# A convolution module on one core: two chunks instead of three on VectorE, GpSimd's splits and sums moved to VectorE

## The chip, the core and the metric

The kernel runs on one core of a Trainium2 chip. The core has TensorE (matrix products into PSUM), VectorE, ScalarE, GpSimd, and SyncE (SP), which issues the DMA transfers. Each engine works through a queue of its own in program order, and semaphores hold an instruction back until what it needs is done. The metric is the device time of one execution in microseconds; lower is better.

## What is computed

The reference is a two-layer trunk over 512 tokens of 1024 features, all in fp32. Layer 0 has a mixer (spatial gating and neighbourhood attention) and a squared-ReLU channel mixer, layer 1 a Conformer convolution module and another channel mixer. The change touches the convolution module alone:

```python
def conformer_conv(h, w_pw1, b_pw1, w_dw, b_dw, ln_g, ln_b, w_pw2, b_pw2):
    a, gate = jnp.split(h @ w_pw1 + b_pw1, 2, axis=-1)
    y = a * jax.nn.sigmoid(gate)
    y = lax.conv_general_dilated(y, w_dw[:, None, :], window_strides=(1,),
                                 padding=[(CONV_K // 2, CONV_K // 2)],
                                 dimension_numbers=('NWC', 'WIO', 'NWC'),
                                 feature_group_count=CONV_W) + b_dw
    y = jax.nn.silu(layernorm(y, ln_g, ln_b))
    return y @ w_pw2 + b_pw2
```

The convolution is depthwise with 31 taps along the tokens; the layer norm behind it needs the mean and variance over all 1024 channels of each token.

## The kernel before

Features lie on the partitions: the 1024 channels are eight chunks of 128, and a chunk is a tile of 128 x 512 tokens. fp32 products are made from two parts, a rounded high part and the remaining low part: `mm3` (L87 to L90) issues high x high, low weight x high, high weight x low. Weights come as 1 MB tiles (`raw`, two buffers, loaded by SP) and are split in four quarters by `Weights.piece`: ScalarE casts the high part `whi` (L93), and VectorE or GpSimd subtracts it for the low part `wlo` (L94); `el` says which. A tile's next load is issued after its last quarter's split, and `raw` is free when that split is done. `chunk` (L218) issues a chunk's 24 matmuls, then up to two quarters of the next tile, then "side work" for VectorE worth so many microseconds (`work`), then the chunk's evacuation from PSUM.

The side work in this stage is the convolution of some chunks on VectorE: the chunks in `VECTOR_CONV` are convolved by 31 multiply-adds each (a "tap", L1125 and L1128), queued in `aux` and drawn by `work` from two chunks in turn. The other chunks are convolved on TensorE (`conv_steps`, L1152): for those, 16 DMA copies of 67.5 KB on SP's queue (L1140) write shifted copies of the padded chunk `ypad` into four tiles `y` (for chunk 7, ten copies by DMA and six by ScalarE, L1138), GpSimd builds matrices of taps (`conv_weights`, L1148) in two buffers, and 32 matmuls with 32 columns each go through them (64 passes of TensorE in the trace).

`glu(c)` makes chunk c of the gated product: two `chunk` calls of 24 matmuls each, ("g", c) evacuated by ScalarE's sigmoid (L1106), ("a", c) by VectorE into `ypad` (L1116). Chunks 0 and 1 are made before `conv_module` begins. Each convolved chunk is centred on `m0` (the mean over the channels of chunk 0) and added to running sums of values and squares by `take` (L1175 to L1184); GpSimd keeps one set of sums for chunks 0 and 4, VectorE another for the rest, and two additions (L1239) merge them. `sums` (L1248) then turns the running sums into statistics with TensorE, and `normed` (L1270 to L1278) norms the chunks as operands of the last product. The order of all this is the order in which `conv_module` is written; there is no planner.

Of the kernel before, what the change touches and what calls it, by code (L numbers as in the profile page):

```python
# [27 lines left out]
VECTOR_CONV = (1, 2, 3)  # L28

# columns of the packed vectors  # L30
# [12 lines left out]
# columns of the shape constants  # L43
# [6 lines left out]
# window of a query tile of 16 columns: first key column, kind of mask  # L50
# [5 lines left out]
def body(ctx: ExitStack, tc: tile.TileContext, I: dict, out: bass.AP):  # L56
# [11 lines left out]
    def nm(s):  # L68
        uid[0] += 1
        return f"{s}_{uid[0]}"  # L70
# [25 lines left out]
    class Pieces:  # L96
        """a weight tile in four pieces of two rows of blocks"""
# [8 lines left out]
    class Weights:  # L106
        """Weight tiles in the order of their use: loaded and split ahead of it, in pieces."""
# [15 lines left out]
        def piece(self, i, q, el=None):  # L123
            """a quarter of a tile, in its two parts"""
# [50 lines left out]
    def work(us):  # L175
        """emit side work worth about us of VectorE time, from two queues in turn"""
        while aux and us > 0:
            queue = aux[0]
            cost, go = queue.popleft()
            go()  # L180
            us -= cost
            if not queue:
                aux.popleft()
            elif len(aux) > 1:
                aux[0], aux[1] = aux[1], aux[0]

    def steps(m, w, c, acts, evac, t0=0, t1=T, ks=range(KC), every=2):
        """one output chunk; yields every few k"""
# [14 lines left out]
    def together(ms, acts, evac, t0=0, t1=T, ks=range(KC), hook=None):  # L203
        """output chunks side by side, k outermost; ms: (id, weight tile, column)"""
# [13 lines left out]
    def chunk(m, w, c, acts, evac, us, ks=range(KC), t0=0, t1=T, np_=2, el=None):  # L218
        """one output chunk, with side work beside it"""
# [59 lines left out]
    def preload(func):  # L279
        """brings in a function's table ahead of its use"""  # L280
        act.activation(small(1, "pre"), epsc, func)
# [4 lines left out]
    class SumSq:  # L286
        """Running sum of squares over feature chunks."""
# [19 lines left out]
        def flush(self):  # L307
            """the last addition, a step behind its square"""
# [16 lines left out]
    def gain(norm, s):  # L325
        """norm_g * (1 + s)"""
# [4 lines left out]
    def modulate(items, r, alt):  # L331
        """items: (source, gain, shift, hi, lo); one item a step, its low part a step later"""
# [25 lines left out]
    # ================= start =========================================  # L358
# [13 lines left out]
    # silu(c) along the free axis, on every partition  # L372
# [11 lines left out]
    # shift and scale of the first norm, for x and for ctx, a quarter of the features at a time;  # L384
    # each row group of the array holds a quarter of the sum
# [135 lines left out]
    # ================= layer 0: mixer ================================  # L521
# [6 lines left out]
    def perm(t):  # L528
        """the (block, row, column) order of a tile, seen in token order"""
# [23 lines left out]
    def first_v():  # L553
        """the first weights of v, where scores and modulation weights go later"""
# [9 lines left out]
    # ctx, normalised and modulated  # L564
# [85 lines left out]
    # bias of a head over the 48 columns around a query tile, then under the three masks  # L650
# [12 lines left out]
    def head_bias(hd, rows):  # L663
        """the table comes back to front: its rows rise with the query, and are read from the end"""
# [12 lines left out]
    # spatial gating  # L677
# [3 lines left out]
    def gelu2(dst, ps, n):  # L681
        """twice gelu(ps), tanh form"""
# [39 lines left out]
    def spatial(gs):  # L722
        """the gate over the tokens"""
# [23 lines left out]
    # attention, for the two heads of a pair and 16 columns of queries at a time  # L747
# [46 lines left out]
    def weigh(u):  # L794
# [12 lines left out]
        if j == 3:  # L807
            # the reciprocals of the sums, along the free axis
# [73 lines left out]
    # the last of the content, and the mixer's halves as operands of the last projection  # L882
# [33 lines left out]
    def norm_between(acts, evac, ss, norm, l, qs, qc, evac_next, ids, third, ks=range(KC),  # L916
                     between=lambda: None, staged=True):
        """the last four chunks of one product, a norm, and the first four chunks of the next one, by token halves;
        third: where the first weights of the next product go; returns the normed operand"""
# [94 lines left out]
    # ================= channel mixer =================================  # L1014
    def mlp(l, lead, us, tail):
        """lead: norm_between without its consumer; tail: what follows the last but two chunks"""
# [25 lines left out]
        def third():  # L1042
            """eight slots of the hidden layer, before they are needed"""
# [37 lines left out]
    def free_gemv():  # L1081
        """the two buffers of the modulation weights, which are done"""
# [5 lines left out]
    # ================= layer 1: convolution module ===================  # L1088
# [13 lines left out]
    def evac_glu(m, ps, t0, t1):  # L1102
# [19 lines left out]
        if c in VECTOR_CONV:  # L1122
# [8 lines left out]
            aux.append(deque(jobs + [(1.8, lambda: take(c, dve))]))  # L1131
# [13 lines left out]
    def conv_weights(c):  # L1145
        n = len(cv["matrices"]) % 2
        wd = cv["matrices"][c] = cv["wd"][:, n * 1024 : n * 1024 + 1024].rearrange("p (a b) -> p a b", b=32)
# [22 lines left out]
    def take(c, e, t0=0, t1=T):  # L1170
        """centre a chunk on m0 and add it to the engine's sums"""
        m0 = cv["m0"]
        lsum, lsq = cv["sums", e is pool]
        z = zs[c][:, t0:t1]
        e.tensor_tensor(z, z, m0[:, t0:t1], op=ALU.subtract)  # L1175
        if (e is pool) not in cv["begun"]:
            cv["begun"].add(e is pool)
            e.tensor_copy(lsum[:, t0:t1], z)
            act.activation(lsq[:, t0:t1], z, AF.Square)
        else:  # L1180
            sq = slot(cols=t1 - t0, s="sq")
            act.activation(sq, z, AF.Square)
            e.tensor_tensor(lsum[:, t0:t1], lsum[:, t0:t1], z, op=ALU.add)
# [318 lines left out]
```

## Time and profile before

| | us |
|---|---|
| median of three runs | 1203.87 |
| lowest and highest run | 1201.37, 1205.72 |
| span of the profiled execution (its run time is not given apart) | 1200.8 |
| TensorE busy in that span | 1157.8 |
| VectorE, ScalarE, GpSimd busy | 761.0, 474.1, 227.5 |

The span runs from the first to the last instruction of one profiled execution. Times of day in the text are microseconds from its start; the convolution stage lies between about 665 and 812. A row of a timeline merges instructions of one kind that follow each other: start, time from the first start to the last end, engine, line, operation, tiles, count, and in brackets the idle time before it with what ended it. Instructions of one engine overlap a little, so a row's time divided by its count is the pace, while a mean of single durations is somewhat longer. Matmul ends are modelled. The granted clock (PEclk) is the share of TensorE's full clock in that stretch.

### The profile page before, as it was taken

To read this page: it belongs to the slowest core of one execution; us is meant where nothing else is said; L and a number is where in the kernel's file an instruction comes from. 1 tells how busy PE (TensorE), PEld (TensorE's weight loads), DVE (VectorE), ACT (ScalarE), POOL (GpSimd) and SP (SyncE) were. 2 spreads that over 40 slices of the span, in tenths; PEclk is the share of its full clock that TensorE was granted. 3 is DMA by queue.
4 is the path that set the end of the run, shared out by engine and by line. 5 is a ranking of instruction groups with operands and counts; after the bars stand their busy time and mean duration, and the time that the engine had idled before them with its cause. 6 is when DMAs were issued, how large, how long until landed. Compare 5 with 4: busy or idle time off the path is not lost.

```text
span 1200.8 us, 16380 instructions
## 1 busy us (share of the span) xinstructions
PE 1157.8 (96%) x6534; PEld 963.4 (80%) x6534; DVE 761.0 (63%) x1251; ACT 474.1 (39%) x940; POOL 227.5 (19%) x194
## 2 busy tenths in 40 slices
PE   6999999999999999999999999699999999999997
PEld 2688889779988888888889766288988888888887
DVE  4685776557775666665757899877743343443445
ACT  4463445444541331332335332366642242332423
POOL 1240325253200000000012476444200000000001
PEclk8999999999999999999999999799999999999998
DMA  9624444143364455455532415204133222332322
GB/s 366 229 77 162 168 168 142 35 169 112 113 221 178 189 210 199 155 206 208 204 115 75 143 48 163 82 19 141 36 105 106 75 102 105 105 99 77 105 71 70
DMA packets 29836, 160.79 MB, mean 134 GB/s; under 512 B 3968, under 2 KB 7552, under 8 KB 11840
## 3 DMA queue, kind: packets, MB, share of 16 engines
q1 hardware_dynamic: 29760, 159.75, 38.1%
q8 instruction: 51, 0.84, 0.3%
q14 instruction: 25, 0.20, 0.1%
HBM read 152.52 MB, written 2.10 MB: 129 GB/s over the span
## 4 chain that ended last, share of the span: by engine, by line
PE 75%; DVE 7%; DMA 3%; POOL 3%; ACT 3%; issue 2%; DVEq 0%; ACTq 0%; POOLq 0%
PE ps L88 20%; PE ps L89 20%; PE ps L90 20%; PE ps L213 3%; PE ps L210 3%; PE ps L211 3%; DMA graw<-in_wmB_dram 2%; POOL wlo L94 2%; DVE graw L505 1%; PE ps L1159 1%; DMA raw<-in_w_ff_dram 1%; PE ps L695 1%; PE ps L696 1%; PE ps L697 1%; PE ps L804 1%
## 5 line engine op out<-in xcount | busy, mean ns | idle before, releaser
L93 ACT CAST whi<-raw 128x512 fp32r<-128x512 f32 x340 | 191.4, 616 | 198.8 <-PE ps L90 180.6
L88 PE MATMUL ps<-hhi,whi 128*128 128x512 f32 x640 | 253.4, 396 | 1.4 <-ACT hhi L341 1.4
L89 PE MATMUL ps<-hhi,wlo 128*128 128x512 f32 x640 | 250.6, 392 | 3.5 <-POOL wlo L94 2.4
L90 PE MATMUL ps<-hlo,whi 128*128 128x512 f32 x640 | 249.9, 390 | 0.0
L94 POOL TENSOR_TENSOR wlo<-raw,whi 128x512 fp32r<-128x512 f32 x84 | 133.6, 1609 | 512.1 <-ACT whi L93 508.5
L90 PE MATMUL ps<-hid,whi 128*128 128x512 f32 (+1 forms) x520 | 196.3, 378 | 0.0
L89 PE MATMUL ps<-hid,wlo 128*128 128x512 f32 (+1 forms) x520 | 196.3, 378 | 0.0
L88 PE MATMUL ps<-hid,whi 128*128 128x512 f32 (+1 forms) x520 | 196.3, 378 | 0.0
L94 DVE TENSOR_TENSOR wlo<-raw,whi 128x512 fp32r<-128x512 f32 x256 | 177.3, 729 | 23.5 <-ACT whi L93 22.8
L910 DVE SCALAR_TENSOR_TENSOR x<-ps,mod,x 128x512 f32<-128x512 f32 (+1 forms) x94 | 62.7, 669 | 156.5 <-PE ps L90 151.2
L88 PEld LDWEIGHTS ps<-hhi,whi 128*128 128x128 f32 x640 | 120.9, 189 | 33.7 <-issue 6.0
L89 PEld LDWEIGHTS ps<-hhi,wlo 128*128 128x128 f32 x640 | 120.8, 189 | 29.4 <-POOL wlo L94 4.4
L90 PEld LDWEIGHTS ps<-hlo,whi 128*128 128x128 f32 x640 | 120.5, 188 | 25.5 <-DVE hlo L349 0.3
L505 DVE CUSTOM_DVE_ANT_0 graw<-graw,cB,vec 128x1024 f32<-128x1024 f32 x80 | 103.6, 1305 | 17.8 <-DMA graw<-in_wmB_dram 17.6
L88 PEld LDWEIGHTS ps<-hid,whi 128*128 128x128 f32 x520 | 97.8, 188 | 18.2
L89 PEld LDWEIGHTS ps<-hid,wlo 128*128 128x128 f32 x520 | 97.8, 188 | 18.2
L90 PEld LDWEIGHTS ps<-hid,whi 128*128 128x128 f32 x520 | 97.8, 188 | 18.1
L1036 DVE TENSOR_TENSOR z<-z 128x512 f32<-128x512 f32 (+1 forms) x72 | 46.4, 651 | 93.8 <-ACT z L1034 93.8
L1034 ACT ACTIVATE z<-ps 128x512 f32<-128x512 f32 (+1 forms) x72 | 38.9, 550 | 138.9 <-PE ps L90 136.3
L1128 DVE SCALAR_TENSOR_TENSOR zc<-ypad,vec,zc 128x512 f32<-128x512 f32 x90 | 86.8, 1009 | 1.1
L1040 DVE TENSOR_TENSOR hid<-z,hid 128x512 fp32r<-128x512 f32 (+1 forms) x72 | 45.7, 641 | 43.3 <-ACT hid L1038 43.3
L1390 POOL TENSOR_TENSOR o<-o,rstd 128x256 f32<-128x256 f32 x2 | 1.9, 950 | 322.2 <-DVE rstd L322 322.2
(264 smaller groups left out, 1749.6 us busy)
## 6 DMA issues: line engine op xcount, KB each, us to landing
raw<-in_w_ff_dram SPq DMA_DIRECT2D x64, 1024.0 KB
graw<-in_wmB_dram SPq DMA_DIRECT2D x40, 1024.0 KB
raw<-in_w_pw_dram SPq DMA_DIRECT2D x12, 1024.0 KB
raw<-in_w_in_dram SPq DMA_DIRECT2D x10, 1024.0 KB
wmA<-in_wmA_dram SPq DMA_DIRECT2D x7, 1024.0 KB
y<-ypad SPq DMA_DIRECT2D x74, 67.5 KB
raw<-in_w_out_dram SPq DMA_DIRECT2D x4, 1024.0 KB
x<-in_xT_dram SPq DMA_DIRECT2D x8, 256.0 KB
```

What stands on the lines that cost most here:

```text
L88: pe.matmul(ps, w[0], a[0], start=first, stop=False)
L89: pe.matmul(ps, w[1], a[0], start=False, stop=False)
L90: pe.matmul(ps, w[0], a[1], start=False, stop=last)
L93: (e or act.copy)(hi, src)
L94: (el or dve).tensor_tensor(lo, src, hi.bitcast(F32), op=ALU.subtract)
L210: pe.matmul(ps, w[0][:, k, c : c + P], a[0], start=n == 0, stop=False)
L505: dve.tensor_tensor_reduce(out=wv, in0=wv, in1=cB, scale=1.0, scalar=vcol(V_BMOD, l * 48 + q * 8 + j % 8), op0=ALU.mult, op1=ALU.add, accu ...
L910: dve.scalar_tensor_tensor(x[:, m, t0:t1], ps, gate[:, m : m + 1], x[:, m, t0:t1], op0=ALU.mult, op1=ALU.add)
L1034: act.activation(z, ps, AF.Relu)
L1036: dve.tensor_tensor(z, z, z, op=ALU.mult)
L1040: dve.tensor_tensor(lo, z, hi.bitcast(F32), op=ALU.subtract)
L1128: dve.scalar_tensor_tensor(z, yt[:, k : k + T], vcol(V_WDW, c * CONV_K + k), z, op0=ALU.mult, op1=ALU.add)
```

## The change

Chunk 3 moves from VectorE's taps to TensorE. GpSimd no longer makes low parts of weights in this module (`el=pool` is dropped in `glu` and behind it), nor centres and sums chunks 0 and 4: VectorE does both, in one set of sums, and the merging additions go. The tap matrices of chunk 7 get a place of their own, `cB`, which held GpSimd's sums. The convolutions are reordered: 3 behind chunk 4's products, 4 and the first half of 5 ahead of chunk 7's products, the second half of 5 behind them. The two extra calls of `work(6)` go, and `work(100)` moves forward. Comments and docstrings are dropped too.

```diff
-VECTOR_CONV = (1, 2, 3)
+VECTOR_CONV = (1, 2)
...
-            aux.append(deque(jobs + [(1.8, lambda: take(c, dve))]))
+            aux.append(deque(jobs + [(1.8, lambda: take(c))]))
...
     def conv_weights(c):
-        n = len(cv["matrices"]) % 2
-        wd = cv["matrices"][c] = cv["wd"][:, n * 1024 : n * 1024 + 1024].rearrange("p (a b) -> p a b", b=32)
+        n = (len(cv["matrices"]) - (7 in cv["matrices"])) % 2
+        wd = cB if c == 7 else cv["wd"][:, n * 1024 : n * 1024 + 1024]
+        wd = cv["matrices"][c] = wd.rearrange("p (a b) -> p a b", b=32)
...
-    def take(c, e, t0=0, t1=T):
-        """centre a chunk on m0 and add it to the engine's sums"""
-        m0 = cv["m0"]
-        lsum, lsq = cv["sums", e is pool]
+    def take(c, t0=0, t1=T):
+
+        lsum, lsq = cv["sums"]
         z = zs[c][:, t0:t1]
-        e.tensor_tensor(z, z, m0[:, t0:t1], op=ALU.subtract)
-        if (e is pool) not in cv["begun"]:
-            cv["begun"].add(e is pool)
-            e.tensor_copy(lsum[:, t0:t1], z)
+        dve.tensor_tensor(z, z, cv["m0"][:, t0:t1], op=ALU.subtract)
+        if not cv["begun"]:
+            cv["begun"] = True
+            dve.tensor_copy(lsum[:, t0:t1], z)
             act.activation(lsq[:, t0:t1], z, AF.Square)
         else:
             sq = slot(cols=t1 - t0, s="sq")
             act.activation(sq, z, AF.Square)
-            e.tensor_tensor(lsum[:, t0:t1], lsum[:, t0:t1], z, op=ALU.add)
-            e.tensor_tensor(lsq[:, t0:t1], lsq[:, t0:t1], sq, op=ALU.add)
+            dve.tensor_tensor(lsum[:, t0:t1], lsum[:, t0:t1], z, op=ALU.add)
+            dve.tensor_tensor(lsq[:, t0:t1], lsq[:, t0:t1], sq, op=ALU.add)
...
         def glu(c):
             w = W.use()
-            chunk(("g", c), w, 0, h, evac_glu, 4.0, el=pool)
-            chunk(("a", c), w, P, h, evac_glu, 4.0, el=pool)
+            chunk(("g", c), w, 0, h, evac_glu, 4.0)
+            chunk(("a", c), w, P, h, evac_glu, 4.0)
             W.free()
...
         conv_weights(0)
-        conv_weights(4)
+        conv_weights(3)
+
...
         glu(3)
         conv_pe(0)
+        conv_weights(4)
+        conv_weights(7)
         biased((2, 3))
-        work(6)
         glu(4)
         cv["m0"] = vp.tile([P, T], F32, name="m0")
         ps = bank()
         colsum(ps, zs[0])
         act.activation(cv["m0"], ps, AF.Copy, scale=1.0 / 128.0)
-        take(0, pool)
+        take(0)
+        conv_pe(3)
+        conv_weights(5)
+        biased((4, 5))
         glu(5)
-        biased((4, 5))
+        take(3)
+        biased((6, 7))
         glu(6)
         conv_pe(4)
-        conv_weights(5)
         conv_weights(6)
-        biased((6, 7))
-        work(6)
-        take(4, pool)
+        conv_pe(5, a0, a1)
+        take(4)
         glu(7)
         preload(AF.Silu)
-        conv_pe(5)
-        conv_weights(7)
-        W.pieces(4, pool)
+        work(100)
+        conv_pe(5, b0, b1)
+        take(5)
+        W.pieces(4)
         conv_pe(6, a0, a1)
-        work(100)
-        take(5, dve)
-        for i in range(2):
-            dve.tensor_tensor(cv["sums", False][i], cv["sums", False][i], cv["sums", True][i], op=ALU.add)
-        lsum, lsq = cv["sums", False]
+        lsum, lsq = cv["sums"]
```

How the instructions move is shown at three places. First, VectorE's queue around the evacuation of chunk 2 into `ypad` (L1116); `zc` is a convolved chunk (here chunks 1 and 2), `wlo` a low part of weights. A piece of the difference:

```order
 L1128 SCALAR_TENSOR_TENSOR zc_5964<-ypad_5859,vec,zc_5964 128x512 x11
 L1116 SCALAR_TENSOR_TENSOR ypad_6040<-ps_6009,vec,sg_6007 128x512
+L94 TENSOR_TENSOR wlo_6073<-raw_5927,whi_6072 128x512 x2
 L1128 SCALAR_TENSOR_TENSOR zc_5964<-ypad_5859,vec,zc_5964 128x512
 L1125 TENSOR_SCALAR zc_6044<-ypad_6040,vec 128x512
```

Two low parts now stand ahead of the taps here, and two more ahead of the next six taps; before, GpSimd had all four.

Second, ScalarE's queue behind the mean `m0` of chunk 0 (`m`), where the high parts `whi` for chunk 6's product are cast. Before:

```order
L1219 ACTIVATE m_6274<-ps_6275 128x512
L1179 ACTIVATE cB<-zc_5936 128x512
L93 CAST whi_6306<-raw_6115 128x512 x2
L1179 ACTIVATE lsum_5970<-zc_5964 128x512
L1106 ACTIVATE sg_6320<-ps_6281,vec 128x512
```

Now:

```order
L1220 ACTIVATE m_6287<-ps_6288 128x512
L1179 ACTIVATE lsum_5970<-zc_5936 128x512
L1162 ACTIVATE zc_6127<-ps_6294,vec 128x512
L1207 ACTIVATE x<-x,bg_5971 128x512 x2
L93 CAST whi_6356<-raw_6115 128x512 x2
```

The casts now stand behind the evacuation of chunk 3's convolution (`zc_6127`) and two bias passes over `x`.

Third, VectorE's queue around the evacuation of chunk 7 (the only L1116 in each piece). Before:

```order
L1184 TENSOR_TENSOR lsum_5970<-lsum_5970,sq_6532 128x512
L1128 SCALAR_TENSOR_TENSOR zc_6127<-ypad_6123,vec,zc_6127 128x512 x12
L1116 SCALAR_TENSOR_TENSOR ypad_6617<-ps_6580,vec,sg_6578 128x512
L1128 SCALAR_TENSOR_TENSOR zc_6127<-ypad_6123,vec,zc_6127 128x512 x7
L1175 TENSOR_TENSOR zc_6127<-zc_6127,m_6274 128x512
```

Now:

```order
L1184 TENSOR_TENSOR lsum_5970<-lsum_5970,sq_6613 128x512
L94 TENSOR_TENSOR wlo_6643<-raw_6399,whi_6642 128x512 x2
L1128 SCALAR_TENSOR_TENSOR zc_6044<-ypad_6040,vec,zc_6044 128x512 x4
L1175 TENSOR_TENSOR zc_6044<-zc_6044,m_6287 128x512
L1183 TENSOR_TENSOR lsum_5969<-lsum_5969,zc_6044 128x512
L1184 TENSOR_TENSOR lsum_5970<-lsum_5970,sq_6653 128x512
L94 TENSOR_TENSOR wlo_6643<-raw_6399,whi_6642 128x512 x2
L1116 SCALAR_TENSOR_TENSOR ypad_6690<-ps_6659,vec,sg_6657 128x512
```

Chunk 3's twelve taps ahead of the evacuation are replaced by four of chunk 2, that chunk's `take` and four low parts, and no tap follows.

## Rows read from the trace of the kernel before

**Rows 1.** The page, part 1: busy us, share of the span, instructions.
```profile
PE 1157.8 (96%) x6534; PEld 963.4 (80%) x6534; DVE 761.0 (63%) x1251; ACT 474.1 (39%) x940; POOL 227.5 (19%) x194
```
**Rows 2.** TensorE's waits from 660 to 830: in total us, times, longest.
```profile
PE ps L1159 <- DMA y<-ypad: 10.8, 3, 9.3
PE ps L89 <- POOL wlo L94: 2.4, 1, 2.4
```
**Rows 3.** Windows: length, busy us (count) of each engine, clock, DMA share, GB/s.
```profile
705.00:710.00 5.00, 2.60 (x10) 1.48 (x9) 5.00 (x7) 0.60 (x1) 5.00 (x2) 1.00 0.00 0
...
760.00:765.00 5.00, 0.18 (x4) 0.00 (x0) 4.82 (x7) 0.00 (x0) 0.00 (x0) 0.76 0.23 97
765.00:770.00 5.00, 0.54 (x2) 0.18 (x2) 4.79 (x8) 4.65 (x7) 0.00 (x0) 0.50 0.34 83
```
**Rows 4.** Timeline of TensorE, 665 to 783.
```profile
665.20 0.40 PE L88 MATMUL ps<-hhi,whi 128*128 128x512 f32 x1
...
687.08 7.07 PE L1159 MATMUL ps<-y,graw 128*32 128x512 f32 x64
...
705.09 1.02 PE L1168 MATMUL ps<-zc,ones 128*128 128x512 f32 x2
...
708.75 0.50 PE L89 MATMUL ps<-hhi,wlo 128*128 128x512 f32 x1 [2.40 <-POOL wlo L94]
...
749.65 10.53 PE L1159 MATMUL ps<-y,graw 128*32 128x512 f32 x128
769.46 1.03 PE L1159 MATMUL ps<-y,graw 128*32 128x256 f32 x2 [9.29 <-DMA y<-ypad]
771.75 1.03 PE L1159 MATMUL ps<-y,graw 128*32 128x256 f32 x2 [1.25 <-DMA y<-ypad]
773.05 8.68 PE L1159 MATMUL ps<-y,graw 128*32 128x256 f32 x124 [0.27 <-DMA y<-ypad]
782.23 1.05 PE L1248 MATMUL ps<-ones,lsum 128*128 128x1 f32 x8 [0.50 <-DVE lsum L1183]
```
**Rows 5.** Timeline of VectorE, 671 to 771.
```profile
671.65 0.54 DVE L1125 TENSOR_SCALAR zc<-ypad,vec 128x512 f32<-128x512 f32 x1
...
692.92 0.74 DVE L1116 SCALAR_TENSOR_TENSOR ypad<-ps,vec,sg 128x512 f32<-128x512 f32 x1
693.58 13.99 DVE L1128 SCALAR_TENSOR_TENSOR zc<-ypad,vec,zc 128x512 f32<-128x512 f32 x21
...
748.95 15.57 DVE L1128 SCALAR_TENSOR_TENSOR zc<-ypad,vec,zc 128x512 f32<-128x512 f32 x12
764.44 0.75 DVE L1116 SCALAR_TENSOR_TENSOR ypad<-ps,vec,sg 128x512 f32<-128x512 f32 x1
765.10 5.47 DVE L1128 SCALAR_TENSOR_TENSOR zc<-ypad,vec,zc 128x512 f32<-128x512 f32 x7
```
**Rows 6.** Timeline of GpSimd: low parts of weights in two stretches.
```profile
696.77 17.03 POOL L94 TENSOR_TENSOR wlo<-raw,whi 128x512 fp32r<-128x512 f32 x4 [10.67 <-ACT whi L93]
...
750.15 6.77 POOL L94 TENSOR_TENSOR wlo<-raw,whi 128x512 fp32r<-128x512 f32 x4
```
**Rows 7.** Groups by line and shape, VectorE, 665 to 790: busy us, mean ns.
```profile
L1128 DVE SCALAR_TENSOR_TENSOR zc<-ypad,vec,zc 128x512 f32<-128x512 f32 x90 | 86.8, 1009 | 1.1
...
L1184 DVE TENSOR_TENSOR lsum<-lsum,sq 128x512 f32<-128x512 f32 x3 | 2.1, 688 | 2.2 <-ACT sq L1182 2.2
```
**Rows 8.** Timeline of SP's queue: issues of the shifted copies of chunks 6 and 7.
```profile
740.27 10.71 SPq L1140 DMA_DIRECT2D y<-ypad  x16
...
765.25 6.21 SPq L1140 DMA_DIRECT2D y<-ypad  x10
```
**Rows 9.** Timeline of ScalarE behind chunk 0's convolution: bias passes, casts.
```profile
694.86 1.32 ACT L1207 ACTIVATE x<-x,bg 128x512 f32<-128x512 f32 x2
696.08 1.13 ACT L93 CAST whi<-raw 128x512 fp32r<-128x512 f32 x2
```

More of the change, by code (lines that the diff above doesn't have):

```diff
@@ L1182, in take @@
             act.activation(sq, z, AF.Square)
-            e.tensor_tensor(lsum[:, t0:t1], lsum[:, t0:t1], z, op=ALU.add)
-            e.tensor_tensor(lsq[:, t0:t1], lsq[:, t0:t1], sq, op=ALU.add)
+            dve.tensor_tensor(lsum[:, t0:t1], lsum[:, t0:t1], z, op=ALU.add)
+            dve.tensor_tensor(lsq[:, t0:t1], lsq[:, t0:t1], sq, op=ALU.add)
     def conv_module(h):
         vp = cv["vp"]
-        cv["sums", False] = tuple(vp.tile([P, T], F32, name=nm("lsum")) for _ in range(2))
-        cv["sums", True] = cB[:, :T], cB[:, T:]
-        cv["begun"] = set()
+        cv["sums"] = tuple(vp.tile([P, T], F32, name=nm("lsum")) for _ in range(2))
+        cv["begun"] = False
         (a0, a1), (b0, b1) = HALVES
@@ L1283, in go @@
                 next(gen, None)
-        take(6, dve, a0, a1)
+        take(6, a0, a1)
         conv_pe(7, a0, a1)
-        take(7, dve, a0, a1)
+        take(7, a0, a1)
         conv_pe(6, b0, b1)
@@ L1293, in conv_module @@
         na = normed(a0, a1)
-        take(6, dve, b0, b1)
+        take(6, b0, b1)
         go(na)
@@ L1300, in conv_module @@
         go(na)
-        take(7, dve, b0, b1)
+        take(7, b0, b1)
         ss = SumSq()
```

## Prediction

> **What bounds the kernel now.** I read the page's busy times first, then TensorE's waits in the convolution stage, then the timelines of the engines there. TensorE is busy 96% of the span, VectorE 63% [rows 1], so over the whole kernel only TensorE's own work and the places where it stands still count. Its waits between 660 and 830 us name two large ones: 10.8 us for DMA copies of `ypad` into `y`, and 2.4 us for a low part of weights from GpSimd [rows 2]. The five-microsecond windows show the same: 2.60 of 5 us busy from 705, then 0.18 and 0.54 of 5 us from 760 to 770, with the granted clock at 0.76 and 0.50, which is the lower of its two levels (1.2 of 2.4 GHz). After the 2.4 us wait the clock was still 1.00 [rows 3].
>
> TensorE's timeline fixes the pace. A GLU chunk pair costs 10.94 us (two of them lie between 665.20 and 687.08), a whole TensorE convolution 7.0 us, a half one 3.5 us (10.53 us for one and a half). After 760.18 it waits for chunk 7's shifted copies, goes on at 769.46, 771.75 and 773.05, and takes 8.68 us for 124 passes that cost about 6.8 at full clock. The sums start at 782.23 [rows 4].
>
> Why so late? Chunk 7 leaves its PSUM bank through VectorE (`ypad`, L1116), and VectorE comes to that at 764.44 though TensorE was done with it by 749.65. Before it stand 12 taps that took 15.57 us; elsewhere 21 taps took 13.99 us [rows 5]. In the slow stretch GpSimd ran four low parts in 6.77 us; in the fast one it was itself held, four taking 17.03 us [rows 6]. All 90 listed taps took 86.8 us, 0.96 each [rows 7], where two chunks in turn run at 0.67 and one chunk alone, whose every tap needs the one before, at 0.78 [rows 5]. So the two engines slow each other, VectorE's queue runs late, and chunk 7 pays at its end.
>
> **The change, part by part.**
>
> *TensorE:* chunk 3's convolution is added, 7.0 us of pure path. From 665.20 to the sums its work is six GLU pairs, 65.6; the column sum, 0.5; whole convolutions of 0, 3, 4, 21.0; halves of 5 (two), 6 (two), 7 (one), 17.5 [rows 4]. That is 104.6 us, with 0.2 for small gaps 770.0, against 782.23: **12.2 us less if TensorE never waits**. Splitting chunk 5 into halves costs nothing by the same row (one and a half took 10.53, a whole one 7.07). The 19.2 us that TensorE loses today thus pay for 7.0 of new work.
>
> *VectorE:* it loses 31 taps and two merging additions. It gains 24 low parts before chunk 7's evacuation (four more after it), and five more operations of `take` for chunks 0 and 4 ahead of that point. Until the evacuation of chunk 7 it has 62 taps, of which 23 stand alone (0.78) and 39 in turn (0.67), 44.0 us; five evacuations at 0.74, 3.7; 24 low parts and 14 operations of `take` at 0.69 (the row of one such 128x512 operation [rows 7]), 26.2. Together 73.9 us from 671.65 [rows 5], to 745.5 without waits. But a low part needs ScalarE's high part, and it now stands in VectorE's one queue with taps behind it. ScalarE makes those casts after the convolution's evacuation and two bias passes (1.32, then 0.57 a cast [rows 9]). For chunk 5's weights VectorE is ready at 693.3 and the cast at 696.7, a wait of 3.4; for chunk 6's, ready at 709.6, cast at 715.6 behind conv 3, a wait of 6.0; later ones add about 1. That gives 755.6. TensorE ends chunk 7 at 756.4, so the two meet: VectorE is ready 0.8 us early. It has little to spare, and I keep that for the rivals.
>
> *Chunk 3's copies:* VectorE reaches chunk 3 at 692.5, as before (692.92 [rows 5]): 12 taps alone, 9.4; 12 in turn, 8.0; one evacuation, 0.7; four low parts, 2.8. Behind it SP issues 16 copies, as for another chunk in 10.71 us [rows 8]; a copy lands 2.3 us after its issue (the first group of chunk 7: fourth issue 767.1, matmul 769.46). Last landing 705.6, while TensorE arrives at 705.5. The wait is between 0 and 2 us (a queue slower by a fifth); I take 0.5, the row's pitch. The 16 issues stand ahead of the weight loads of chunk 7 and push those to about 704; their casts come after 728, so they are covered.
>
> *Chunk 7's copies:* ten issues in 6.21 us, the rest by ScalarE. Before, the first group served 5.0 us after the start of the evacuation and the last 8.6 us after it (764.44 to 769.46 and 773.05). From 756.4 that gives 765.0. TensorE has now the second half of 5 and the first of 6 in between and arrives at 763.4: a wait of 1.6 to 1.8, I take 1.8. Bounds 1 and 3.5: the weight load issued just before can hold the copies, as the longer pitch of 0.67 against 0.62 suggests [rows 8]. The 2.4 us wait kept the clock at 1.00 [rows 3], so I charge no lower clock.
>
> *GpSimd:* it keeps the tap matrices (one more, chunk 7's into `cB`) and the padding; nobody waits for them, since 5's matrix is made right after conv 3 and used some 29 us later. ScalarE's work is unchanged in kind. After the sums the order is the old one on every engine.
>
> **Sum.** 12.2 - 0.5 - 1.8 = **9.9 us less**, span 1190.9 for 1200.8. The page gives no run time of the profiled execution itself; the median of the three runs, 1203.87, is 3.1 above its span, and I move that median: **1194.0 us**. With both bounds, 12.2 - 1 = 11.2 and 12.2 - 5.5 = 6.7, that case spans 1192.7 to 1197.2, and the three runs lie 2.5 below and 1.9 above their median.
>
> **Rivals.** *First, VectorE still arrives late by a few microseconds.* The margin of 0.8 us is small, and each microsecond of further waiting for ScalarE's casts goes straight into chunk 7's wait. Two to five microseconds more leave a gain of 4.9 to 7.9, 1196 to 1199. For it: the queue is strictly in order, and one wait for a cast is already 6.0. Against: those waits eat slack that the sum already holds.
>
> *Second, the exchange is a wash.* VectorE takes over what GpSimd did and is no earlier at chunk 7: evacuation at 764.44, copies at 773.0, sums at 782.2, and the added convolution only fills idle time: 1203.9. For it: GpSimd's work was not free before, each engine stretched the other. Against: over 748.95 to 764.44 VectorE lost 7.5 us (15.57 against 12 at 0.67) to GpSimd, and four low parts cost it 2.8. The Trainium skill, Perfetto Trace Analysis, section Optimizing Scalar/DVE Operations, says that offloading between GpSimd and VectorE might not help, because they share an SBUF port. By that rule the time would be this rival's 1203.9; the row above speaks for a gain, 7.5 against 2.8.
>
> *Third, slower: VectorE becomes the bound.* If the stretch of the taps is not GpSimd's doing, VectorE's 73.9 us run at 0.96/0.71 (mean pitch before against the mix of 0.67 and 0.78), a factor of 1.36: 100.5 us, chunk 7 at 772.2, 7.7 later than 764.44 and the sums with it: 1211.6. It decides from a factor of 1.26, where 73.9 us fill the 92.8 us from 671.65 to 764.44. For it: the taps' mean. Against: the 21 taps in 13.99, and 7 taps alone in 5.47 with GpSimd idle [rows 5].
>
> **Chances.** Forecast 0.64, first rival 0.20, second 0.10, third 0.06. A measurement of this kernel tells 0.3% (3.6 us) from no change: faster 0.84, within it 0.10, slower 0.06. The range leaves out the second and third rivals and a little of each end: 1190.5 (best bound less the runs' scatter) to 1199.5 (the first rival at five microseconds).
>
> **What would show it.** Right: the wait for `y` falls from 10.8 to 1 to 4 us, the one for GpSimd's `wlo` is gone, the clock stays 1.00 from 700 to 790; taps at 0.67 to 0.78; chunk 7's `ypad` between 755 and 758; sums between 771 and 775, the rest of the span unchanged at 418.6. VectorE shows waits for `whi` of about 3 and 6 us ahead of low parts. Wrong: chunk 7's `ypad` after 760, a new wait of TensorE for VectorE's `wlo`, or for chunk 3's `y` over 2 us; taps still near 1 us with GpSimd idle would be the third rival.

## The result, and the profile after

The changed kernel takes 1194.55 us (median of five runs, 1192.50 to 1197.54), against 1203.87 before (five runs, 1201.37 to 1207.20): ratio 0.9924, 95% interval 0.9905 to 0.9943. The forecast was 1194.0 in a range of 1190.5 to 1199.5.

| us | before | after |
|---|---|---|
| span of the profiled execution | 1200.8 | 1192.8 |
| stage: first matmul of chunk 0's convolution to first matmul of the sums | 95.15 | 86.05 |
| VectorE evacuates chunk 7, from the same start | 77.36 | 69.68 |
| from the sums to the end of the span | 418.6 | 417.9 |

In the profiled execution after, the stage starts 1.8 us later than before (688.88 for 687.08), though the code ahead of it is the same in both. So the stage, not the span, is the measure in all that follows. It fell by 9.1 us; 9.9 were forecast. The median fell by 9.3. Some line numbers are shifted by one (L1159 is now L1160, L1168 is L1169), and by a few in the experiments.

The page, part 1, against [rows 1]: TensorE is busy 4.7 us longer (chunk 3's convolution is 7.07, and what the lower clock stretched before is gone), GpSimd 53.8 us less, VectorE 30.5 us less.

```profile
PE 1162.5 (97%) x6662; PEld 968.6 (81%) x6662; DVE 730.5 (61%) x1248; ACT 475.5 (40%) x942; POOL 173.7 (15%) x166
```

TensorE's waits from 660 to 830, against [rows 2], in total us, times, longest: the 10.8 us for `y` are 1.4, and the wait for GpSimd's low part is gone.

```profile
PE ps L1160 <- DMA y<-ypad: 1.4, 2, 0.7
PE ps L317 <- DVE acc L311: 0.8, 1, 0.8
PE ps L1260 <- DVE zc L1270: 0.5, 1, 0.5
```

Windows, with the columns of [rows 3]. The first row is the stretch from chunk 0's convolution to the evacuation of chunk 7: TensorE is busy in all of it, and VectorE in 54.73 of 69.66 us. The second row is VectorE's, from its first tap to its being ready for chunk 7. Around 765, where the clock stood at 0.50 before, it stays at 1.00.

```profile
688.90:758.56 69.66, 69.66 (x455) 44.32 (x458) 54.73 (x79) 20.62 (x36) 8.01 (x12) 1.00 0.45 126
673.45:757.18 83.73, 83.73 (x515) 55.94 (x514) 69.78 (x103) 24.82 (x43) 8.01 (x12) 1.00 0.45 126
...
760.00:765.00 5.00, 5.00 (x100) 3.03 (x96) 0.00 (x0) 4.90 (x9) 0.00 (x0) 1.00 0.61 199
765.00:770.00 5.00, 3.62 (x56) 1.99 (x52) 4.76 (x8) 3.24 (x7) 0.00 (x0) 1.00 0.24 59
```

TensorE's timeline, against [rows 4]. The convolution of chunk 3 is the new 7.07 us at 707.85; the three waits ahead of chunk 7's convolution have shrunk to two short ones.

```profile
688.88 7.08 PE L1160 MATMUL ps<-y,graw 128*32 128x512 f32 x64
...
706.90 1.02 PE L1169 MATMUL ps<-zc,ones 128*128 128x512 f32 x2
707.85 7.07 PE L1160 MATMUL ps<-y,graw 128*32 128x512 f32 x64
...
765.33 0.59 PE L1160 MATMUL ps<-y,cB 128*32 128x256 f32 x2
766.59 0.59 PE L1160 MATMUL ps<-y,cB 128*32 128x256 f32 x2 [0.67 <-DMA y<-ypad]
767.89 3.43 PE L1160 MATMUL ps<-y,cB 128*32 128x256 f32 x58 [0.71 <-DMA y<-ypad]
...
774.93 1.05 PE L1248 MATMUL ps<-ones,lsum 128*128 128x1 f32 x8
```

VectorE's timeline, against [rows 5]. Six taps in turn take 4.05 us, 0.67 each. The price of the strict queue are the waits for ScalarE's casts, 4.41 and 5.48 us. At chunk 7 VectorE now waits for TensorE, 1.38 us.

```profile
674.02 8.62 DVE L1128 SCALAR_TENSOR_TENSOR zc<-ypad,vec,zc 128x512 f32<-128x512 f32 x11
...
698.53 2.61 DVE L94 TENSOR_TENSOR wlo<-raw,whi 128x512 fp32r<-128x512 f32 x2 [4.41 <-ACT whi L93]
701.06 4.05 DVE L1128 SCALAR_TENSOR_TENSOR zc<-ypad,vec,zc 128x512 f32<-128x512 f32 x6
...
717.49 1.29 DVE L94 TENSOR_TENSOR wlo<-raw,whi 128x512 fp32r<-128x512 f32 x2 [5.48 <-ACT whi L93]
...
758.56 0.75 DVE L1116 SCALAR_TENSOR_TENSOR ypad<-ps,vec,sg 128x512 f32<-128x512 f32 x1 [1.38 <-PE ps L90]
```

VectorE's groups: from 665 to 785, 60 listed taps in 42.4 us, 0.71 each, where 90 took 86.8 us before [rows 7]; from 673.9 to 757.2, 20 low parts.

```profile
L1128 DVE SCALAR_TENSOR_TENSOR zc<-ypad,vec,zc 128x512 f32<-128x512 f32 x60 | 42.4, 746 | 0.7
...
L94 DVE TENSOR_TENSOR wlo<-raw,whi 128x512 fp32r<-128x512 f32 x20 | 14.2, 750 | 11.3 <-ACT whi L93 11.3
```

### The profile page after: what moved, and what is told of

Its sections match the earlier page's. It is cut to its first block, busy times and chain, and to the rows that moved or that the text cites. A ratio compares the mean times of both kernels' runs of the same rounds, so it can differ in the third digit from the quotient of the medians.

```text
span 1192.8 us, 16638 instructions
## 1 busy us (share of the span) xinstructions
PE 1162.5 (97%) x6662; PEld 968.6 (81%) x6662; DVE 730.5 (61%) x1248; ACT 475.5 (40%) x942; POOL 173.7 (15%) x166
## 4 chain that ended last, share of the span: by engine, by line
PE 80%; DVE 6%; DMA 3%; ACT 2%; issue 1%; POOL 1%; DVEq 0%; SPq 0%; ACTq 0%; POOLq 0%
PE ps L88 21%; PE ps L89 21%; PE ps L90 21%; PE ps L1160 3%; PE ps L213 3%; PE ps L210 3%; PE ps L211 3%; DMA graw<-in_wmB_dram 2%; DVE graw L505 1%; DMA raw<-in_w_ff_dram 1%; PE ps L695 1%; PE ps L804 1%; PE ps L696 1%; PE ps L697 1%; ACT s L775 1%
## 5 line engine op out<-in xcount | busy, mean ns | idle before, releaser
L94 DVE TENSOR_TENSOR wlo<-raw,whi 128x512 fp32r<-128x512 f32 x280 | 193.7, 728 | 34.8 <-ACT whi L93 34.0
L94 POOL TENSOR_TENSOR wlo<-raw,whi 128x512 fp32r<-128x512 f32 x60 | 86.1, 1449 | 478.1 <-ACT whi L93 477.6
L1038 ACT CAST hid<-z 128x512 fp32r<-128x512 f32 (+1 forms) x72 | 40.6, 572 | 51.7 <-DVE z L1036 51.7
```

The source lines that it names most:

```text
L94: (el or dve).tensor_tensor(lo, src, hi.bitcast(F32), op=ALU.subtract)
L1038: act.copy(hi, z)
```

## The experiments

The change has two halves: GpSimd's work goes to VectorE, and chunk 3 goes from VectorE to TensorE in a new order. The theory at the start of the experiments was that the gain needs both. All stages below run from the first matmul of chunk 0's convolution to the first of the sums.

### One half at a time

**GpSimd's work to VectorE, three chunks and the old order kept.**

```diff
-            chunk(("g", c), w, 0, h, evac_glu, 4.0, el=pool)
-            chunk(("a", c), w, P, h, evac_glu, 4.0, el=pool)
+            chunk(("g", c), w, 0, h, evac_glu, 4.0)
+            chunk(("a", c), w, P, h, evac_glu, 4.0)
...
-        take(0, pool)
+        take(0, dve)
...
-        take(4, pool)
+        take(4, dve)
...
-        W.pieces(4, pool)
+        W.pieces(4)
```

The merging additions go too.

> The kernel before with one half of the change alone: GpSimd's low parts, centring and sums go to VectorE, but VectorE keeps three chunks and the old order stays. Measure: the stage from the first matmul of chunk 0's convolution to the first matmul of the sums (95.15 us before, 86.05 changed). Theory (the gain needs both halves): no tap is stretched any more (0.67 to 0.78 a tap), but VectorE has some 86 taps, 59.8 us, five evacuations, 3.7, and 35 operations at 0.69, 24.2, so 87.7 us and 3 to 6 us of waits for casts ahead of chunk 7, which leaves at 762 to 766 as before (764.4): stage 92 to 96, ratio 0.996 to 1.002. Rival 1 (GpSimd's slowing of VectorE was the whole matter): chunk 7 by 758, the stage 88 or less, ratio 0.992 or less even with three chunks. Rival 2 (the two engines don't slow each other): taps stay at 0.96, VectorE needs about 111 us, chunk 7 after 780, ratio above 1.01.

Measured: ratio 1.000 (0.9989 to 1.0011), stage 93.26. In the windows VectorE is busy 70.08 of 71.78 us up to chunk 7, 6.8 less than the 76.91 of 77.44 before. Chunk 7 leaves 5.5 us earlier (71.81 for 77.36). But then VectorE waits for casts, which stand behind ScalarE's copies for chunk 7 and a table load, with seven taps behind the wait, and the sums wait for VectorE. So ratio and stage are the theory's, its reason is not: on the clock of the kernel before, chunk 7 left at 758.9, not at 762 to 766, near the 758 of rival 1, and the gain was lost behind it. The windows of the kernel before and of this run, and VectorE's and TensorE's timelines of this run:

```profile
687.00:764.44 77.44, 70.65 (x451) 43.98 (x450) 76.91 (x82) 18.86 (x33) 50.41 (x32) 0.99 0.39 111
```

```profile
690.80:762.58 71.78, 69.91 (x451) 44.20 (x450) 70.08 (x101) 18.96 (x33) 10.94 (x5) 1.00 0.41 120
```

```profile
762.58 0.74 DVE L1116 SCALAR_TENSOR_TENSOR ypad<-ps,vec,sg 128x512 f32<-128x512 f32 x1
769.93 2.50 DVE L94 TENSOR_TENSOR wlo<-raw,whi 128x512 fp32r<-128x512 f32 x4 [6.60 <-ACT whi L93]
772.34 5.47 DVE L1128 SCALAR_TENSOR_TENSOR zc<-ypad,vec,zc 128x512 f32<-128x512 f32 x7
...
784.03 1.06 PE L1246 MATMUL ps<-ones,lsum 128*128 128x1 f32 x8 [3.63 <-DVE lsum L1183]
```

**Chunk 3 to TensorE and the new order, GpSimd's work kept on GpSimd.** The edit gives the changed kernel `el=pool` and the two sets of sums back; `cB` holds sums again, so chunk 7's matrix goes behind chunk 5's convolution.

```diff
-        take(0)
+        take(0, pool)
...
-        take(5)
-        W.pieces(4)
+        conv_weights(7)
+        take(5, dve)
+        W.pieces(4, pool)
```

> The changed kernel with the other half alone: two chunks on VectorE and the new order, but GpSimd makes the low parts in the GLU again and centres and sums chunks 0 and 4 in sums of its own (chunk 7's matrix then goes behind chunk 5's convolution). Theory (the gain needs both halves): taps are stretched again, to about 0.96, but 62 of them take only 59.5 us, with evacuations 3.7 and six sums 4.1 about 67 us of the 85 that there are, so chunk 7 still leaves on time (757 to 760). What comes back is TensorE's wait for GpSimd's low parts: four per weight tile at 1.7 to 4.3 us behind the tap matrices in GpSimd's queue, 2 to 6 us in all; stage 88 to 92, ratio 0.994 to 0.998. Rival 1 (fewer taps alone make the gain): no wait for low parts over 1 us, stage 86 to 87, ratio 0.992. Rival 2 (the stretch decides): chunk 7 after 762 again, stage 95 or more, ratio 1.000 or above.

Measured: ratio 0.9917 (0.9895 to 0.9939), stage 86.98: as fast as the whole change. The theory missed, rival 1 holds. The taps are stretched as before, 60 in 57.4 us against 42.4, but VectorE is no busier up to chunk 7 (55.91 of 69.76 us, 54.73 in the changed kernel), since the low parts are not on it. It was ready 62.78 us after the stage's start and waited 7.00 us for TensorE; in the changed kernel it was ready after 68.30. GpSimd's low parts cost TensorE nothing: its waits name no `wlo`. Of the new order, only the place of chunk 5's convolution was tried apart (below). The window, the group and the row of VectorE's timeline at chunk 7:

```profile
686.50:756.26 69.76, 69.76 (x459) 44.39 (x461) 55.91 (x59) 20.64 (x36) 45.31 (x32) 1.00 0.45 125
```

```profile
L1128 DVE SCALAR_TENSOR_TENSOR zc<-ypad,vec,zc 128x512 f32<-128x512 f32 x60 | 57.4, 998 | 0.7
```

```profile
756.26 0.75 DVE L1116 SCALAR_TENSOR_TENSOR ypad<-ps,vec,sg 128x512 f32<-128x512 f32 x1 [7.00 <-PE ps L90]
```

**Only the low parts back on GpSimd** (`el=pool` in `glu` and behind it).

> The changed kernel with only the low parts of the GLU's weights back on GpSimd; centring and sums stay on VectorE in one set. Theory: VectorE has 24 operations less and longer taps, chunk 7 on time; TensorE waits for GpSimd's low parts as in the run with all of GpSimd's work, 1 to 5 us: stage 87.5 to 91, ratio 0.993 to 0.997. It tells which part of GpSimd's work costs: if the low parts are it, this run is within 1 us of the run with all of it; if the centring and sums are it, this one is within 1 us of the changed kernel (86.05).

Measured: ratio 0.9923 (0.9901 to 0.9945), stage 86.66. No wait of TensorE for a low part, so the theory missed here too; the three variants of the changed kernel lie within 1 us.

**Chunk 5's convolution whole behind chunk 7.**

```diff
-        conv_pe(5, a0, a1)
...
-        conv_pe(5, b0, b1)
+        conv_pe(5)
```

> The changed kernel with chunk 5's convolution whole behind chunk 7's products, as before, instead of one half ahead of them. TensorE has the same work, but 7.0 us in place of 3.5 between chunk 7's end and its need, and half of chunk 6 besides. Theory (the two halves cost nothing and win nothing, VectorE sets chunk 7's evacuation): VectorE is ready at 757.1 in any case, 1.4 us earlier than TensorE let it be, so chunk 7's copies come 1.4 us earlier and the waits for them, 0.67 and 0.71, shrink by about as much: stage 84.6 to 86, ratio 0.990 to 0.993. Rival (the new order of chunk 5 is part of the gain, as VectorE would be late): chunk 7 after 760, the wait for its copies over 3 us, stage 88 or more.

Measured: ratio 0.9907 (0.9885 to 0.9929), stage 85.00. VectorE evacuates chunk 7 at 67.08 instead of 69.68: 2.6 us earlier where 1.4 were expected, since VectorE, no longer held 1.13 us by a square of ScalarE, was itself ready 1.2 us earlier. One wait of 0.95 for `y` is left. The split of chunk 5 was no part of the gain; undoing it wins 1 us.

### Where the first half's gain went

**The low parts behind the last taps**, on top of the first run:

```diff
-        W.pieces(4)
         conv_pe(6, a0, a1)
         work(100)
         take(5, dve)
+        W.pieces(4)
```

> The kernel before with GpSimd's work on VectorE (the first run), and one more edit: the low parts of the next weights stand behind the last taps and the centring of chunk 5 instead of ahead of them. Theory: that run let chunk 7 leave 5.5 us earlier than before and gave it back, because VectorE then waited 6.60 us for ScalarE's casts, which stand behind ScalarE's six copies and its table load, with seven taps behind the wait, and the sums waited 3.6 us for VectorE. With the low parts moved the wait of the sums goes: stage 93.26 - 3.6 = 89.7, between 89 and 91, ratio 0.995 to 0.998. Rival (the sums are late for another reason, or the low parts are now late for the last product): stage 92 or more, ratio above 0.999.

Measured: ratio 0.9941 (0.9922 to 0.9959), stage 89.68. The wait of the sums is gone, and the exchange alone is worth 5.5 us of the stage, without any new work on TensorE. The changed kernel too has these low parts behind chunk 5's centring, so this run, not the first, shows the exchange as the change has it. What remains is 8.1 us of waits for `y` and the lower clock behind them (0.50 in the window from 770 to 775).

**Half of chunk 3's taps left out**, once with GpSimd's work as before, once with the edits of the last run:

```diff
-            jobs = [(0.7, lambda k=k: tap(k)) for k in range(CONV_K)]
+            jobs = [(0.7, lambda k=k: tap(k)) for k in range(16 if c == 3 else CONV_K)]
```

> The kernel before, GpSimd's work and the order as they were, with chunk 3's last 15 of 31 taps left out (that part of its convolution is not computed). It takes away half of one chunk's load from VectorE and adds nothing to TensorE. Theory (the load on VectorE decides, as the run with GpSimd's work kept suggests): 15 taps at 0.96 are 14.4 us, so VectorE reaches chunk 7 at 750, as soon as TensorE is done with it (749.65); its copies are there by 759 and TensorE, which comes at 760.18, does not wait; the clock does not fall. Stage (first matmul of chunk 0's convolution to the first of the sums) 80 to 83 instead of 95.15, ratio 0.986 to 0.990; the difference to the changed kernel's 86.05 would be the added convolution on TensorE less its own waits. Rival (GpSimd's work beside the taps holds chunk 7 back whatever the number of taps): chunk 7 after 757, stage 88 or more, ratio 0.995 or above.

Measured: ratio 0.9961 (0.9948 to 0.9973), stage 90.60. Chunk 7 left at 69.82, 7.5 us earlier, not 14.4. Ratio and stage are the rival's, but not its reason, since chunk 7 did move with the number of taps. The theory's count was wrong: seven of chunk 3's taps stand behind chunk 7 before [rows 5], so the cut takes eight from ahead of it, and chunk 3's centring, 2 us, moves ahead. And then a new hold: the padding of chunk 7 and the load of the next weights stood behind GpSimd's low parts. VectorE evacuated at 756.90, but the copies were issued from 760.40, 3.5 us later where 0.8 stood before (764.44 to 765.25). The chain of waits (start, us, what), then rows of the timeline:

```profile
758.65 1.28 POOL wlo L94
759.93 0.03 POOL ypad L1112
759.96 5.59 DMA raw<-in_w_pw_dram
...
766.76 2.05 DMA y<-ypad
```

```profile
757.42 2.51 POOL L94 TENSOR_TENSOR wlo<-raw,whi 128x512 fp32r<-128x512 f32 x2 [3.89 <-ACT whi L93]
...
759.86 0.12 POOL L1112 MEMSET ypad<- 128x15 f32 x1
...
760.06 3.90 ACT L1138 COPY y<-ypad 32x540 f32<-32x540 f32 x6 [2.19 <-POOL ypad L1113]
760.40 6.94 SPq L1140 DMA_DIRECT2D y<-ypad  x10
```

> The kernel with three chunks on VectorE, GpSimd's work on VectorE and the low parts later, with chunk 3's last 15 of 31 taps left out (that part of its convolution is not computed). Without VectorE's added work the same cut moved chunk 7 only from 77.4 to 69.8 us after the first matmul of chunk 0's convolution, and its copies then still waited 3.1 us for the padding and the weight load behind GpSimd's low parts: stage 90.6. Theory (what is left of that run's wait is GpSimd's queue): here nothing of GpSimd stands ahead of chunk 7, 15 taps at 0.67 are 10 us, VectorE reaches chunk 7 by 62 to 63 us, as soon as TensorE is done with it, its copies are there by 72, TensorE comes at 73 and does not wait: stage 80 to 81.5, ratio 0.985 to 0.988. Rival (chunk 7's copies need the long way in any case): a wait for them of 3 us or more, stage 84 or more.

Measured: ratio 0.9923 (0.9906 to 0.9941), stage 83.96. TensorE could use the first copies 7.0 us after the evacuation began (755.53 to 762.52), where that had been 10.2 with GpSimd's queue ahead of them (756.90 to 767.12). But chunk 7 left at 66.64, not 62 to 63, for the same miscount of taps, and waits of 4.2 us for `y` remained, so the stage is the rival's.

### What GpSimd's work costs VectorE

Twelve operations, or thirty fills, that nobody needs:

```diff
         biased((6, 7))
         glu(6)
+        spare = vp.tile([P, T], F32, name="spare")
+        for _ in range(12):
+            pool.tensor_tensor(spare, kon[:, 0:T], kon[:, 256 : 256 + T], op=ALU.subtract)
```

```diff
+        for _ in range(30):
+            pool.memset(spare, 0.0)
```

> The changed kernel with twelve more operations on GpSimd that nobody needs, in the stretch in which VectorE convolves chunks 1 and 2 (after about 717): each reads two tiles of 128x512 and writes one, as a low part does. Theory (an operation of GpSimd with two inputs takes from VectorE about what VectorE would need to do it itself): each costs VectorE 0.6 to 0.7 us, as 24 low parts, two tap matrices more and five sums cost 60 taps 15 us in the run with GpSimd's work kept; taps beside them at 0.9 to 1.5, VectorE 7 to 8 us later at chunk 7, whose evacuation goes from 69.7 us after the first matmul of chunk 0's convolution to 75 to 77, stage 91 to 93. Rival (the engines don't hinder each other, the taps' mean came from something else): taps at 0.67 to 0.70, stage 86.

> As the run before it, with thirty fills of a 128x512 tile in place of the twelve two-input operations: GpSimd is busy in the same stretch, but reads nothing. Theory (it is GpSimd's reading that hinders VectorE): taps stay at 0.67 to 0.70 beside the fills, stage 86 to 86.5. Rival (any work of GpSimd on the same memory hinders it): taps at 0.9 or more, stage 89 or more.

Measured, one execution each: stage 97.80 with the reads (1206.69 us), 86.42 with the fills (1193.43). With the reads chunk 7 left at 79.28, and both it and the stage lie beyond what the theory expected (75 to 77, 91 to 93). GpSimd's and VectorE's timelines with the reads, then with the fills:

```profile
717.60 19.87 POOL L1231 TENSOR_TENSOR spare<-kon 128x512 f32<-128x512 f32 x12
...
717.88 3.26 DVE L94 TENSOR_TENSOR wlo<-raw,whi 128x512 fp32r<-128x512 f32 x2 [5.47 <-ACT whi L93]
721.06 10.23 DVE L1128 SCALAR_TENSOR_TENSOR zc<-ypad,vec,zc 128x512 f32<-128x512 f32 x6
```

```profile
715.61 17.51 POOL L1231 MEMSET spare<- 128x512 f32 x30
...
715.91 1.29 DVE L94 TENSOR_TENSOR wlo<-raw,whi 128x512 fp32r<-128x512 f32 x2 [5.47 <-ACT whi L93]
717.13 4.06 DVE L1128 SCALAR_TENSOR_TENSOR zc<-ypad,vec,zc 128x512 f32<-128x512 f32 x6
```

Twelve taps and four low parts took 22.8 us with the reads (717.88 to 740.66) and 10.5 with the fills (715.91 to 726.37): 1.0 us lost for each operation that reads, more than the 0.6 to 0.7 expected, nothing for a fill. So it is GpSimd's reading that stretches the taps. The reads delayed VectorE so far that TensorE also waited 3.7 us for a low part. The Trainium skill, SBUF — State Buffer, section Who interferes with whom, says that a VectorE instruction with two inputs from SBUF contends with a GpSimd instruction that reads SBUF and not with one that only writes it; these two runs agree.

### Towards a better kernel

**Four of chunk 7's ten copies by SP given to GpSimd**, with chunk 5 late:

```diff
                     if c == 7 and 4 * g + u > 9:
                         act.copy(to, of)
+                    elif c == 7 and 4 * g + u > 5:
+                        pool.tensor_copy(to, of)
```

> The changed kernel with chunk 5's convolution whole behind chunk 7, and four of chunk 7's ten copies by SP's queue given to GpSimd, which is idle there. Theory (the ten issues in a row set when the last copy lands): SP's sixth issue is done 4.1 us after the first, GpSimd's four copies take 2.4 to 6 us, ScalarE's six 3.9; all are there before TensorE comes at 765.5, the wait of 0.95 goes: stage 84.0 (85.0 without), ratio 0.988 to 0.992. Rival (the landing time or VectorE's evacuation sets it, not the issues): wait 0.7 or more, stage 84.7 to 86.

Measured: ratio 0.9899 (0.9878 to 0.9920), stage 83.43, no wait for `y` left. The four copies took 2.67 us on GpSimd, six issues 3.70 us.

**Chunk 7's last seven taps on VectorE besides.** The partial sum, less `m0`, is made behind the evacuation, and `take(7)` adds it instead of subtracting `m0`.

```diff
+            if c == 7:
+                zt = cv["tail"] = vp.tile([P, T], F32, name="ztail")
+                for k in range(24, CONV_K):
+                    dve.scalar_tensor_tensor(zt, yt[:, k : k + T], vcol(V_WDW, c * CONV_K + k), cv["m0"] if k == 24 else zt,
+                                             op0=ALU.mult, op1=ALU.subtract if k == 24 else ALU.add)
...
-        for k in range(8):
+        ks = 6 if c == 7 else 8
+        for k in range(ks):
```

> As the run before, and chunk 7's taps 24 to 30 on VectorE, straight from the padded chunk, in the 6.10 us in which VectorE waits for ScalarE there; TensorE's convolution of chunk 7 then has six steps of eight. Theory: seven taps in a chain at 0.78 are 5.5 us and fit into the wait; TensorE saves a quarter of 7.0 us, 0.9 ahead of the first sums and 0.9 behind them: stage 83.1, ratio 0.987 to 0.990, the best so far. Rival (VectorE is late for the sums instead): a wait of the sums for VectorE of 1 us or more, stage 84 or more, no gain on the run before.

Measured: ratio 0.9889 (0.9872 to 0.9906), 1190.81 us, stage 82.56. The taps fill the wait, and the 0.9 us ahead of the sums came. Behind the sums TensorE now runs out of convolution to cover the norm, and a new wait eats the other 0.9 us: from the first matmul of the sums to the first of the last product it takes 6.91 us here and in the run before. VectorE's timeline, and TensorE's waits from 655 to 835:

```profile
754.62 1.20 DVE L1147 SCALAR_TENSOR_TENSOR ztail<-ypad,vec,m 128x512 f32<-128x512 f32 x1
755.85 5.44 DVE L1147 SCALAR_TENSOR_TENSOR ztail<-ypad,vec,ztail 128x512 f32<-128x512 f32 x6
```

```profile
PE ps L210 <- ACT chhi L93: 1.0, 1, 1.0
```

This is the lowest ratio of the kernels here; its interval overlaps widely with that of the run before, so of their difference only the stage tells. Against the changed kernel, timed in another series, the two intervals just touch.

**Chunk 4's last seven taps there too**, by the same code behind `take(0)`:

```diff
         take(0)
+        tail(4, cv["y"][4])
         conv_pe(3)
```

Here `tail` holds the lines above, and chunk 4's convolution on TensorE too has six steps.

> As the run with chunk 7's last taps on VectorE, and chunk 4's taps 24 to 30 there too, in the 5.48 us in which VectorE waits for casts behind chunk 0's centring; TensorE's convolution of chunk 4 then has six steps of eight. Theory (TensorE's own work bounds the stage now, and VectorE's wait is free): seven taps are 5.4 us and fill the wait, TensorE saves 1.75 us and VectorE comes to chunk 7 as before: stage 82.56 - 1.75 = 80.8, ratio 0.986 to 0.989. Rival (VectorE's wait was not free, it is late for chunk 7): a wait for chunk 7's copies of 1 us or more, stage 82 or more.

Measured: ratio 0.9906 (0.9887 to 0.9925), no gain on the run before that these times can tell. No profile of this kernel is on record that can be set beside the others (the one taken spans 2980.4 us), so the stage is not known, and whether VectorE was late is open.

The kernels that compute the whole convolution and have a stage, in us from the first matmul of chunk 0's convolution:

| kernel | chunk 7 evacuated | stage | ratio |
|---|---|---|---|
| before | 77.36 | 95.15 | 1 |
| three chunks, GpSimd's work on VectorE | 71.81 | 93.26 | 1.000 |
| the same, low parts later | 71.83 | 89.68 | 0.994 |
| two chunks, GpSimd keeps its work | 69.78 | 86.98 | 0.992 |
| the change, low parts alone on GpSimd | 69.78 | 86.66 | 0.992 |
| the change | 69.68 | 86.05 | 0.992 |
| the change, chunk 5 late | 67.08 | 85.00 | 0.991 |
| and GpSimd copies four | 67.06 | 83.43 | 0.990 |
| and chunk 7's tail on VectorE | 67.05 | 82.56 | 0.989 |

## Why the prediction was right, and where its reason was not

**TensorE's floor: right.** It was to reach chunk 7's convolution 76.3 us after chunk 0's (687.08 to 763.4) and came after 76.45. Chunk 3's convolution cost its 7.07 us. The 0.5 us put down for its copies came, by luck, from elsewhere: the convolution starts 0.95 us behind the column sum, whose pace is 0.46 (705.09 to 705.55 before), but it does so too with the low parts on GpSimd, where SP's last issue ended 2.3 us ahead of it instead of 3.7, and no wait for `y` is named there. What makes this gap is open.

**Chunk 7's copies: the term that was too small.** 1.8 us were put down, bounds 1 and 3.5. From TensorE's arrival (765.33) to the sums passed 9.60 us for 7.0 of work: 2.6 lost, of which the profile names 1.4 as waits for `y`. TensorE could use the last copies 9.3 us after the evacuation began instead of 8.6, and ten issues took 6.90 us where 6.21 stood before [rows 8]. This 0.8 is the whole difference between 9.9 and 9.1. The prediction named the likely reason, the weight load issued just before, but only for its upper bound. In the three runs whose load was issued 6.8 to 8.3 us ahead of the ten copies (the kernel before, and the two with three whole chunks and GpSimd's work on VectorE), the issues took 6.21 us; in the eight with 0.4 to 2.6 us between, the changed kernel (2.2) among them, 6.65 to 7.73. No run moved the load alone.

**VectorE's time: right as a sum, by luck.** It was to be ready for chunk 7 83.9 us after its first tap, and was after 83.7 (673.45 to 757.18). Two errors cancel in that. The prediction counted 24 low parts ahead of chunk 7 where 20 stand, so that VectorE was busy 69.8 us and not 73.9; and it was idle 13.95 us and not 10.4. The two large waits for casts were 4.41 and 5.48 for a forecast of 3.4 and 6.0, the rest 4.1 for 1. (The terms as written add to 755.9, not 755.6, which leaves a margin of 0.5.) TensorE was done with chunk 7 1.38 us later; 0.8 had been the margin. The clock stayed at 1.00, as expected.

**The reason for VectorE's lateness: half wrong.** The prediction took from one stretch that GpSimd cost VectorE 7.5 us where four low parts would cost 2.8, and so held the exchange for a good part of the remedy. That is true of three chunks: there the exchange takes 6.8 us off VectorE (76.91 to 70.08), chunk 7 leaves 5.5 us earlier, and with the low parts placed as in the change the stage falls by 5.5. It is not true of the change as it is: with two chunks the exchange takes 1.2 us off VectorE (55.91 to 54.73), and waits for casts come on top, 15.2 us in the changed kernel for 3.9 with GpSimd's work kept (VectorE's waits for `whi` from 655 to 785). VectorE is ready for chunk 7 5.5 us later with the exchange than without it (68.30 for 62.78), and TensorE, done with chunk 7 at 69.7, hides that. So the exchange, left out of the change, costs nothing measurable: chunk 3's move with the new order gives the gain without it. The stretch of 15 us over 60 taps is real, but there VectorE spends about as much on GpSimd's work when it does it itself. The number came out right because it rested on TensorE's floor and on VectorE being ready in time, which holds either way.

**The time: partly luck too.** The forecast put the median 3.1 us above the span. In every run that has both on record the time is 1.8 us above the span, so the profiled execution before was, by this estimate, a run of 1202.6, 1.3 us below the median. The span after is 1192.8 for a forecast of 1190.9, mostly because the stage started 1.8 us later; the two errors nearly cancel, and 1194.55 stands against 1194.0.

**The rivals.** The first (VectorE late) did not come. The second took the whole change for a wash. For the exchange alone its time came once (1.000), but not its mechanism: chunk 7 was earlier, and the gain was lost at the sums. The Trainium skill, Perfetto Trace Analysis, section Optimizing Scalar/DVE Operations, warns that offloading between GpSimd and VectorE might not help. With two chunks on VectorE that is what the runs show (0.9917 without the exchange, 0.9924 with it); with three it helped, once the low parts stood later (0.994). The prediction weighed that sentence against the change as a whole, and missed that it bore on one half. The third needed taps near 1 us with GpSimd idle; they ran at 0.67 to 0.78.

The two halves don't add: the exchange with the low parts placed right gives 5.5 us, chunk 3's move 8.2, both 9.1. Both shorten the same wait, and with chunk 3 moved VectorE is ahead of TensorE already, so the exchange has no more to win there.

## What to carry to other kernels

When a change moves work in two ways, price each half by itself over the whole stretch up to the wait, not by its worst place, and price it beside the other half: taking GpSimd's work won VectorE 6.8 us with three chunks on it and 1.2 with two. A microsecond won at an engine's queue is kept only if the next wait in that queue, here for casts behind another engine's copies, is moved too. Where the bound engine still waits a little, look for idle time of the others just there (GpSimd's 2.67 us of copies, VectorE's seven taps) before moving more work to it.

## What the runs showed of the hardware that was not expected

- An operation of GpSimd that reads two 128x512 tiles took 1.0 us from VectorE's two-input work for each of the twelve; thirty fills of the same tile, in 17.51 us beside the same taps, took nothing (4.06 us for six taps either way).
- GpSimd copied a 32x540 piece to other partitions in 0.67 us (2.67 for four), about ScalarE's pace (3.90 us for six); beside VectorE's seven taps of chunk 7 the same four took 3.75.
- GpSimd's matrices took 1.92 us each alone, and one took 9.01 us beside twelve taps that kept their 0.67 us, in the run with GpSimd's work kept (693.78 to 702.79). Later in that run twelve taps took 16.14 us beside GpSimd's work. So which of the two engines is held changes from place to place.
- Ten issues of copies by SP took 6.21 us where the weight load before them was 6.8 us or more old, and 6.65 to 7.73 where it was 0.4 to 2.6 us old (eleven runs; no run changed that alone).
